# Which queue issues the writes of kept weights, of chunk 1's partial sums and of the recurrence's output: hybrid decoder step on one Trainium2 core

## Chip, cores and metric

One Trainium2 chip, one of its cores. The metric is the device time of one execution in microseconds (us); lower is better. Several executions are timed, and one more is recorded by the hardware profiler.

## What is computed

One inference step of a one-layer decoder. 1024 prompt tokens (and 64 sample tokens with a state and a cache) go through a normalisation and one joint projection into an RWKV-7 time-mixing group and a sliding-window attention group. Both outputs are gated, put side by side and projected back, then a gated per-layer embedding is added. The reference, cut to what matters:

```python
def step(S, inp):                       # RWKV-7, one token
    r_t, w_t, k_t, v_t, kk_t, a_t = inp
    sa = jnp.einsum('bhvk,bhk->bhv', S, kk_t)
    S = (S * w_t[:, :, None, :] - sa[..., None] * (kk_t * a_t)[:, :, None, :]
         + v_t[..., None] * k_t[:, :, None, :])
    return S, jnp.einsum('bhvk,bhk->bhv', S, r_t)
...
mixed = jnp.concatenate([o_r * jax.nn.silu(gate_r), o_a * jax.nn.silu(gate_a)], axis=-1)
h = h + mixed @ w_out
gate = jax.nn.sigmoid(rmsnorm(h, g_ple) @ w_pg)
h = h + gate * (p @ w_pp)
```

## The kernel before

The prompt's tokens are held as three column chunks, `CH`: 384, 384 and 320 columns (the last holds 256 prompt tokens and the 64 sample tokens). All matrix products are done in float32 with each operand split in a high and a low part, so each product is three matmuls. The kernel is written with a tile framework that puts the instructions of each engine in order itself, by a timeline that it works out before the kernel is built; a change of one operation's queue can so move others on every engine.

Up to about 520 us of the execution the joint projection and the attention run. Then `chain` lets generators take turns. `prepare` (line 772) makes, for a group of four 64-token blocks, what the recurrence needs: Gram matrices, masks, a triangular solve on VectorE (DVE; tiles `ti`, `tm`, `a`) with a detour through DRAM (`at_d`, lines 842 and 844; `tt_d`), and `TE`/`TF` (lines 883, 891), whose result ScalarE (ACT) scales into the tile `B` at line 894. `steps` (line 948) runs the recurrence block by block: matmuls at lines 962, 967, 974, 987, 990 with small DVE and ACT operations between (`rh` line 964, `sv` lines 968 and 969). `finish` (line 918) normalises a group's outputs, transposes each block's (`ytr`, line 942), copies it on ACT into a tile `or` (line 945, one buffer only) and writes that to DRAM (`or_d`, line 946): 17 writes of 128 KB, one for each of the 16 blocks of the prompt and one for the sample. The next copy at line 945 has to wait until the write before it has landed, since the tile has one buffer.

Beside this runs `Late`. Its `first` multiplies the attention half by the output weights `woa` for chunks 0 and 1; chunk 1's sums are written to `hxa` in DRAM (line 1230, eight writes of 192 KB) and loaded again later (line 1175). `second` (line 1239) does the recurrence's half with the weights `wor`, after loading `or_d` (line 1154) and `sg_d`; `gate` (line 1321) multiplies by the gate weights `wg` and the embedding weights `wpp`. A weight is loaded raw (line 143), cast to its high part `wh_..` by ACT (line 146), and its low part `wl_..` is made by GpSimd (POOL; line 55). Then `keep` (line 1301) writes both parts to DRAM at line 1304, and for a later chunk `kept` (line 1306) loads them from there (line 1309; for `wor` the load is line 1272): 16 writes for `woa` and `wor` and 16 for `wg`, all of 512 KB, and 16 for `wpp`, of 128 KB.

Every DMA of these parts goes through `DMAQ(group)` (line 87), which picks the issuing engine from the table `DQ` (line 319): "S" is SyncE (SP), "A" is ACT, and a group not in the table is "S". Before the change the table has one entry, `lp`, the three loads of `p` at lines 1164 and 1167. SP issues 615 DMAs and does nothing else.

Each queue issues in its own order, and an instruction that waits holds all behind it. The framework has eight completion semaphores for DMAs, given out in turn to all of them in the order of the program, whichever engine issues; a DMA is issued only once the one before it on the same semaphore has landed. So at most eight are under way at a time.

Of the kernel before, what the change touches and what calls it, by code (L numbers as in the profile page):

```python
# [39 lines left out]
def _build(ctx, nc, tc, A, O):  # L40
# [45 lines left out]
    global DMAQ  # L86
    DMAQ = lambda g: {"S": nc.sync, "A": nc.scalar, "P": nc.gpsimd}[DQ.get(g, "S")]
    if WARM:
# [227 lines left out]
    e.ast.close()  # L316


DQ = {"lp": "A"}
WARM = 1  # L320
TAIL = 1
RING2 = 0
# [775 lines left out]
class Late:  # L1098
# [202 lines left out]
    def keep(self, w, dst):  # L1301

        for x, d in zip(w, dst):
            DMAQ("wk").dma_start(d, self.e.f32(x))

    def kept(self, name, src, K=8, pool=None, bufs=2):
        w = [(pool or self.e.wp).tile([128, K, 128], F32R, tag=f"w{x}{K}", name=f"w{x}_{name}", bufs=bufs) for x in "hl"]
# [198 lines left out]
```

## Time and profile before

| | |
|---|---|
| time, median of 3 runs | 939.41 us (935.97 to 939.56) |
| the profiled execution | 942.16 us, its span 940.4 us |
| mean granted TensorE clock | 0.937 of full speed |
| TensorE (PE) busy | 828.5 us (88%) |
| VectorE (DVE) busy | 632.7 us (67%) |
| ScalarE (ACT) busy | 372.5 us (40%) |
| GpSimd (POOL) busy | 369.3 us (39%) |
| moved by DMA | 157.81 MB, mean 168 GB/s |

The profiled execution lies 2.75 us above the median of the three runs. An engine's busy time leaves out its DMA issues; those stand in the rows as SPq or ACTq, the sequencer of SP or ACT. "L946" is line 946. "DMA or_d<-or" is a transfer that writes `or_d` from the tile `or`, and its time in the chain of waits runs from the issue to the landing.

### The profile page before, as it was taken

The numbers are of one execution on the slowest core, as the hardware profiler recorded it, in microseconds if no ns is written. First come the engines' busy times: TensorE is split into PE (matmuls) and PEld (weight loads), VectorE is DVE, ScalarE is ACT, GpSimd is POOL, SyncE is SP. The second block draws the span as 40 slices with busy tenths as digits, with TensorE's granted clock in tenths as the row PEclk, the third lists the DMA queues.
The fourth block names the chain that finished last, engine by engine and source line by source line (L and its number), as shares of the span: only waits on it lengthen the run. The fifth ranks groups of instructions, "written<-read, shape, count | busy, mean of one in ns | idle before, by whom it ended". The sixth has DMA issues, their size and how long they took to land.

```text
span 940.4 us, 17475 instructions
## 1 busy us (share of the span) xinstructions
PE 828.5 (88%) x6352; PEld 738.4 (79%) x6352; DVE 632.7 (67%) x1511; ACT 372.5 (40%) x864; POOL 369.3 (39%) x494
## 2 busy tenths in 40 slices
PE   6978999999998989899799965987687989999994
PEld 5878999878886679788688854876577887899983
DVE  7856487777777453468774769588959766854464
ACT  6202086666666442652233332511333443322131
POOL 8548466665676422314231314315433353200000
PEclk9989999999999999899899975899797999999996
DMA  8013201322135447647644499686556879998882
GB/s 292 23 61 101 66 23 57 91 91 77 59 91 156 112 94 167 169 127 171 163 118 123 117 258 316 140 267 182 174 148 223 292 274 329 306 328 278 272 294 82
DMA packets 146007, 157.81 MB, mean 168 GB/s; under 512 B 59288, under 2 KB 115864, under 8 KB 145656
## 3 DMA queue, kind: packets, MB, share of 16 engines
q1 hardware_dynamic: 145104, 155.57, 54.6%
q10 hardware_dynamic: 816, 1.11, 0.4%
q8 instruction: 50, 0.82, 0.4%
q14 instruction: 37, 0.30, 0.1%
HBM read 106.77 MB, written 49.67 MB: 166 GB/s over the span
## 4 chain that ended last, share of the span: by engine, by line
PE 43%; DVE 25%; DMA 14%; ACT 6%; issue 6%; SPq 4%; POOL 2%; DVEq 0%; ACTq 0%; POOLq 0%
PE acc_z L157 6%; PE acc_gr L157 4%; PE acc_q L157 3%; DVE ti L55 3%; PE pp L1348 2%; DVE tm L55 2%; DMA a<-at_d 2%; ACT s L425 2%; PE ov L446 2%; PE acc_wg0g L157 1%; PE acc_wg3g L157 1%; DVE xl L58 1%; PE acc_wg7g L157 1%; PE acc_wg4g L157 1%; DVE s L421 1%
## 5 line engine op out<-in xcount | busy, mean ns | idle before, releaser
L157 PE MATMUL acc_z<-xh,wh_z 128*128 128x384 f32 (+1 forms) x312 | 65.1, 340 | 0.0
L157 PE MATMUL acc_z<-xl,wh_z 128*128 128x384 f32 (+1 forms) x312 | 62.6, 331 | 0.0
L157 PE MATMUL acc_z<-xh,wl_z 128*128 128x384 f32 (+1 forms) x312 | 62.5, 331 | 0.0
L157 PEld LDWEIGHTS acc_z<-xh,wh_z 128*128 128x128 f32 x312 | 53.7, 192 | 1.7 <-ACT pTS L505 0.2
L157 PEld LDWEIGHTS acc_z<-xh,wl_z 128*128 128x128 f32 x312 | 52.3, 188 | 1.0 <-issue 0.2
L157 PEld LDWEIGHTS acc_z<-xl,wh_z 128*128 128x128 f32 x312 | 52.6, 189 | 0.5
L55 DVE TENSOR_TENSOR ti<-ti,tm 128x56 f32<-128x56 f32 (+28 forms) x152 | 50.2, 330 | 3.5
L55 DVE TENSOR_TENSOR tm<-a,ti 128x56 f32<-128x56 f32 (+28 forms) x152 | 50.2, 330 | 3.5
L55 POOL TENSOR_TENSOR sg<-sv,GC 64x256 f32<-64x256 f32 x32 | 20.9, 652 | 63.0 <-DVE sv L55 61.1
L64 POOL TENSOR_SCALAR s<-s,sm 128x256 f32<-128x256 f32 (+1 forms) x64 | 34.6, 557 | 17.2 <-ACT pT L444 4.6
L1187 ACT ACTIVATE q<-hx 128x384 f32<-128x384 f32 (+1 forms) x41 | 20.8, 507 | 51.8 <-DVE hx L55 19.4
L800 PE MATMUL gram<-L,K 64*128 64x128 f32 x272 | 31.4, 324 | 4.9 <-issue 3.3
L55 POOL TENSOR_TENSOR wl_z<-wr_z,wh_z 128x1024 fp32r<-128x1024 f32 x13 | 31.3, 2406 | 10.1 <-ACT wh_z L146 4.8
L800 PEld LDWEIGHTS gram<-L,K 64*128 64x128 f32 x272 | 27.0, 219 | 9.5 <-issue 6.5
L55 DVE TENSOR_TENSOR zr<-acc_z,R 128x384 f32<-128x384 f32 (+2 forms) x52 | 21.7, 434 | 18.5 <-PE acc_z L157 18.2
L55 DVE TENSOR_TENSOR sq<-sq,q 128x384 f32<-128x384 f32 (+1 forms) x41 | 22.6, 552 | 15.1 <-ACT q L1187 14.7
L425 ACT ACTIVATE s<-s,sm 128x256 f32<-128x256 f32 (+1 forms) x64 | 30.9, 485 | 1.9 <-DVE sm L62 1.9
L446 PE MATMUL ov<-pT,vtok 128*64 128x512 f32 x60 | 31.2, 638 | 0.4 <-ACT pT L444 0.4
L1358 ACT ACTIVATE t<-t 128x384 f32<-128x384 f32 (+3 forms) x25 | 12.2, 494 | 46.8 <-DVE t L55 46.8
L55 POOL TENSOR_TENSOR gsa<-gsa,goa 128x384 f32<-128x384 f32 (+1 forms) x12 | 11.8, 985 | 45.8 <-DVE ti L55 27.0
L804 ACT COPY B<-L 64x512 f32<-64x512 f32 x34 | 20.9, 616 | 20.8 <-DVE L L55 19.9
L55 DVE TENSOR_TENSOR L<-gram,cst 128x512 f32<-128x512 f32 x34 | 22.5, 684 | 8.2 <-PE gram L800 8.0
(622 smaller groups left out, 2445.7 us busy)
## 6 DMA issues: line engine op xcount, KB each, us to landing
wr_z<-in_wz SPq DMA_DIRECT2D x13, 512.0 KB
L<-kq_d SPq DMA_DIRECT2D x24, 256.0 KB
sv<-vt_d SPq DMA_DIRECT2D x32, 128.0 KB
wh_wo<-wo_dh SPq DMA_DIRECT2D x8, 512.0 KB
wl_wo<-wo_dl SPq DMA_DIRECT2D x8, 512.0 KB
raw<-in_xT SPq DMA_DIRECT2D x8, 384.0 KB
kq_d<-KQ SPq DMA_DIRECT2D x8, 384.0 KB
bk_d<-BK SPq DMA_DIRECT2D x8, 384.0 KB
```

Of the source, the lines that this page charges most:

```text
L55: e.tensor_tensor(out, a, b, op=op)
L58: V.scalar_tensor_tensor(out, a, s, b, op0, op1)
L64: e.tensor_scalar(out, a, s1, s2, op0, op1)
L157: PE.matmul(acc[:, :n], w_[:, k0 + k, :], a_[c][:, k, :n], start=i + k == 0, stop=i == 2 and k == K - 1)
L421: V.tensor_tensor_reduce(s[:, j, :nk], sc[:, jj, :nk], mask, 1.0, -3e38, ADD, MAX, mx[:, j:j + 1])
L425: S.activation(s[:, j, :nk], s[:, j, :nk], AF.Exp, bias=m[:, 0, j:j + 1], accum_out=m[:, 2, j:j + 1])
L446: PE.matmul(ov[own, :], vtok[:, blk, own], pT[g].rearrange("p a b -> p (a b)"), start=pos == 0, stop=pos == nb - 1)
L800: PE.matmul(Gp[h][:, p], bk[hs, p], L[h][hs, p], start=True, stop=True)
L804: S.copy(r.B[hs, ci], L[h][hs])
L1187: e.S.square(q, h)
L1348: PE.matmul(pa, w[:, i], p[:, i], start=i + j == 0, stop=i == 1 and j == len(pr) - 1)
L1358: S.activation(t, t, AF.Tanh, scale=0.5)
```

## The change

Three groups of DMAs get the entry "A" in the table: `xs` (line 1230), `or` (line 946) and `wkw`, a new name that the writes at line 1304 get in place of `wk`. The loads that kept the name `wk` (lines 1272 and 1309) stay on SP.

```diff
-DQ = {"lp": "A"}
+DQ = {"lp": "A", "wkw": "A", "xs": "A", "or": "A"}
...
         for x, d in zip(w, dst):
-            DMAQ("wk").dma_start(d, self.e.f32(x))
+            DMAQ("wkw").dma_start(d, self.e.f32(x))
```

73 DMAs go from SP to ACT: 48 at line 1304, 8 at line 1230, 17 at line 946. What is computed, and every byte that is moved, stays. The order of the engines up to about 535 us of the execution stays too; behind that it changes on all five.

SP's order around 534 to 548 us of the execution, where the first four outputs of the recurrence are written (`L_` are loads of keys and queries, `sv_` of values, `at_d` and `a_2` the solve's detour):

```order
 L903 DMA sv_5176<-vt_d 64x2x256 x2
-L946 DMA or_d_3664<-or_4773 512x1x64
-L788 DMA L_3688<-kq_d 64x2x512
-L842 DMA at_d_3675<-B_3690 32x16x32 x3
-L946 DMA or_d_3664<-or_4785 512x1x64
-L842 DMA at_d_3675<-B_3690 32x16x32
+L788 DMA L_3688<-kq_d 64x2x512
+L842 DMA at_d_3675<-B_3690 32x16x32 x4
 L937 DMA bvl_5348<-vt_d 128x256
 L937 DMA bvl_5360<-vt_d 128x256
 L793 DMA K_3685<-bk_d 128x2x512
-L946 DMA or_d_3664<-or_4797 512x1x64
```

The writes of `or_d` are gone from SP, and the loads and the writes of `at_d` follow each other directly.

ACT's order at the same place:

```order
 L945 COPY or_4773<-ytr_4770 128x256
 L804 COPY B_3690<-L_3688 64x512
+L946 DMA or_d_3664<-or_4773 512x1x64
 L297 ACTIVATE gtr_6768<-gsr_6767 128x320
 L914 ACTIVATE yq_5140<-y_5135 128x256
 L945 COPY or_4785<-ytr_4782 128x256
+L946 DMA or_d_3664<-or_4785 512x1x64
 L297 ACTIVATE gtr_6799<-gsr_6798 128x320
 L945 COPY or_4797<-ytr_4794 128x256
+L946 DMA or_d_3664<-or_4797 512x1x64
```

Each write now stands behind its own copy on the engine that made it.

ACT's order about 660 to 680 us, where the last group of blocks (12 to 15) of the prompt gets ready for the recurrence (`es` is taken from `TE`, and line 894 makes `B` from `TF`; `sv_5882` is block 12's):

```order
 L886 COPY es_5589<-TE_5590 32x512 x2
-L914 ACTIVATE yq_5846<-y_5841 128x256
-L1136 CAST mrh_7757<-or_7769 128x384
-L894 ACTIVATE B_3686<-TF_5627 32x16x32 x2
-L1136 CAST mrh_7757<-or_7769 128x384
-L819 COPY K_6819<-ktr_6847 128x512
-L914 ACTIVATE yq_5908<-y_5903 128x256
-L968 ACTIVATE sv_5882<-ch_7134 64x256
 L1184 ACTIVATE sq_7781<-hx_6823 128x384
 L1199 ACTIVATE uh_7779<-hx_6823,par 128x384
 L146 CAST wh_wor4c_7876<-wr_wor4c_7874 128x1024
```

and the rows that follow these:

```order
+L1304 DMA wo_dh<-wh_wor4c_7876 128x2x512
+L1187 ACTIVATE q_7823<-hx_6823 128x384
+L1199 ACTIVATE uh_7779<-hx_6823,par 128x384
+L894 ACTIVATE B_3686<-TF_5627 32x16x32 x2
 L945 COPY or_5937<-ytr_5934 128x256
+L946 DMA or_d_3665<-or_5937 512x1x64
+L968 ACTIVATE sv_5882<-ch_7134 64x256
```

Line 894 stood right behind `es` and ahead of the cast of `wor4`; now it stands behind that cast and behind a write of its result.

## Rows read from the trace of the kernel before

**Rows 1.** The page: busy time by engine, and the chain's shares.

```profile
PE 828.5 (88%) x6352; PEld 738.4 (79%) x6352; DVE 632.7 (67%) x1511; ACT 372.5 (40%) x864; POOL 369.3 (39%) x494
...
PE 43%; DVE 25%; DMA 14%; ACT 6%; issue 6%; SPq 4%; POOL 2%; DVEq 0%; ACTq 0%; POOLq 0%
```

**Rows 2.** Windows: length, busy PE, PEld, DVE, ACT, POOL, clock, DMA share, GB/s.

```profile
560.00:600.00 40.00, 27.00 (x174) 23.26 (x174) 34.71 (x85) 17.10 (x37) 17.84 (x24) 0.62 0.85 257
...
800.00:860.00 60.00, 57.45 (x351) 54.40 (x351) 37.31 (x89) 17.36 (x38) 9.18 (x13) 1.00 0.91 311
```

**Rows 3.** Timeline of SP's queue from 534 to 548 us: start, us.

```profile
536.10 0.56 SPq L946 DMA_DIRECT2D or_d<-or  x1
...
540.00 0.55 SPq L946 DMA_DIRECT2D or_d<-or  x1
...
542.83 0.56 SPq L946 DMA_DIRECT2D or_d<-or  x1
...
545.47 0.60 SPq L844 DMA_DIRECT2D a<-at_d  x1
...
547.38 0.55 SPq L946 DMA_DIRECT2D or_d<-or  x1
```

**Rows 4.** Chain of waits from 530 to 560 us: start, us, what.

```profile
536.10 3.41 DMA or_d<-or
...
540.00 2.30 DMA or_d<-or
...
545.47 4.86 DMA a<-at_d
...
558.30 5.42 DMA hx<-in_xT
```

**Rows 5.** The chain from 560 to 700 us.

```profile
564.83 9.06 DMA wo_dh<-wh_woa
573.90 5.08 DMA sv<-vt_d
...
598.46 0.53 SPq L946
...
612.91 0.42 SPq L1230
...
691.57 0.55 SPq L946
```

**Rows 6.** Lines 946, 1304 and 1230: issue, ns min/median/max, first and last start.

```profile
L946 SPq DMA_DIRECT2D or_d<-or x17: 524/552/1444, 536.1 to 785.6; - x17
...
L1304 SPq DMA_DIRECT2D wo_dl<-wl_woa x4: 377/394/460, 568.0 to 626.8; - x4
...
L1304 SPq DMA_DIRECT2D wg_dh<-wh_wg0g x1: 333/333/333, 716.6 to 716.6; - x1
...
L1230 SPq DMA_DIRECT2D hxa<-xr x8: 327/418/1217, 609.5 to 656.3; - x8
```

**Rows 7.** Waits of SP's queue from 500 us: in total, times, longest.

```profile
SPq L1304 <- ACT wh_wor4c L146: 9.3, 1, 9.3
...
SPq L903 <- DMA wo_dh<-wh_woa: 2.2, 2, 1.6
```

**Rows 8.** Waits of ACT from 500 us.

```profile
ACT or L945 <- DMA or_d<-or: 11.7, 7, 2.2
```

**Rows 9.** Waits of PE from 560 to 590 us.

```profile
PE ytr L942 <- DVE y L55: 5.2, 1, 5.2
PE acc_wa L157 <- DVE mal L55: 3.3, 2, 2.4
PE gram L800 <- issue: 3.3, 1, 3.3
```

**Rows 10.** Timeline of ACT from 645 to 712 us.

```profile
666.61 1.19 ACT L894 ACTIVATE B<-TF 32x512 f32<-32x512 f32 x2
...
678.24 1.03 ACT L146 CAST wh_wor4c<-wr_wor4c 128x1024 fp32r<-128x1024 f32 x1
```

## The prediction

> **What bounds the kernel now.** I read the page first: PE is busy for 88% of the span and holds 43% of the chain of waits, DVE 25%, transfers 14%, ACT 6%, SP's own queue 4% [rows 1]. So no engine that the change touches is the bound over the whole; what the change is worth has to come from stretches. The windows show which. Before about 535 us nothing is reordered. From 800 to 860 us PE is busy for 57.45 of 60 us at full clock [rows 2]: what comes earlier there is only worth something if it was late before. From 560 to 600 us PE is busy for 27.0 of 40, the granted clock is 0.62, and the transfers take 0.85 of the DMA engines at 257 GB/s [rows 2]: there PE starves. The chain of waits then shows what is late in such stretches. Around 540 us it runs through the writes of `or_d` and on through SP's queue to a load of `a` at 545.47, and at 558.30 it passes to a load of `hx` [rows 4]; then it stands on transfers of 9.06 and 5.08 us [rows 5]. From there to 700 us it is mostly DVE and PE, with single issues of SP in between [rows 5]. The reader is to see that SP matters in a few places, for a few tenths of a microsecond to two microseconds each, and bytes in one.
>
> **The change part by part.** 73 DMAs move, none is added, no byte is saved. At the durations that SP needs for them, with one row standing for its group, this is 17 x 0.552 + 8 x 0.418 + 16 x 0.394 + 32 x 0.333 = 29.7 us of issue that leaves SP and comes to ACT [rows 6]. ACT is busy for 372.5 us of 940 [rows 1], so it has room; but it is an engine on whose order others wait, SP is not.
>
> *The train around 540 us.* The load of `a` at 545.47 is in the chain [rows 4], and SP issues back to back from 536 to 546 us; ahead of it stand three writes of `or_d`, at 536.10, 540.00 and 542.83, with 0.56, 0.55 and 0.56 us [rows 3] and some 0.07 us from one issue to the next. All three leave: 1.67 + 0.2 = 1.9 us earlier, **-1.9**. The fourth write, at 547.38, stands behind the load and counts for nothing. What the load releases (DVE, then SP's train to the load of `hx` at 558.30) shifts along. Were something else late next, as the landing of the `at_d` writes in the same train, nothing would be gained: bounds 0 and -1.9. I take the whole, since these writes follow each other closer too once the first two are gone.
>
> *The writes of `or_d` themselves.* The single buffer makes each copy at line 945 wait for the write before it, 11.7 us in 7 waits [rows 8]. The first write landed after 3.41 us among SP's loads, the next after 2.30 us [rows 4]. On ACT a write is issued right behind its copy. I count the difference once, **-1.1**, because only around 540 us do these landings stand in the chain with PE behind them; bounds 0 and -11.7.
>
> *Later single issues.* In the chain SP's issue of a moved write stands at 598.46, 612.91 and 691.57 us, with 0.53, 0.42 and 0.55 us [rows 5]. They leave SP's queue, and the load or write behind each comes earlier by as much: **-1.5**. At 691.57 the issue is on the way to a load too, so the gain holds whoever issues the write; bounds 0 and -1.5.
>
> *The first weights kept.* From 564 to 576 us the four parts of `woa` are written among loads. SP's loads of values (line 903) wait for a `wo_dh` write to land, 2.2 us in two waits [rows 7], because the completion semaphore comes round to them. The eight semaphores stay, so a wait of this kind can only be dealt out afresh. I take half, **-1.1**; bounds 0 and -2.2.
>
> *ACT.* The added issues and what they wait for hold all behind them. Issue alone: 29.7 us, of which what lies on the path counts. The nearest row is ACT's share of the chain, 6% [rows 1]: 0.06 x 29.7 = **+1.8**; bounds 0 and +29.7. The largest wait that SP had for a moved write was 9.3 us for the cast of `wor4` [rows 7]; on ACT that cast stands right ahead of the write, so this wait vanishes instead of moving. Writes of low parts wait for POOL, and on ACT that holds casts and copies; the windows show POOL with 17.84 of 40 us busy where it is fullest of the two shown [rows 2], and I count nothing more for it, bounds 0 and one copy of a low part.
>
> *The new order.* From 654 to 760 us all engines get another order. I take 0: PE's work is the same, and what is put later makes room for weights' products put earlier. The bounds are rival two's price on one side and, on the other, the PE waits that could close.
>
> Sum: -1.9 - 1.1 - 1.5 - 1.1 + 1.8 = **-3.8 us**. The profiled execution took 942.16 us, 2.75 above the median of 939.41; it would come to 938.4, and from the median the forecast is **935.6 us** (-0.4%). A measurement of this kernel tells about 0.5%, or 4.7 us, from no change.
>
> **The rivals.** *One: nothing arrives.* Bytes and the eight semaphores bound the stretch from 560 to 600 us, PE and DVE the rest, so what SP saves is waited for elsewhere and ACT's cost eats the remainder. For it: 0.85 of the DMA engines busy [rows 2] and the small share of SP in the chain [rows 1]. Against it: the train of 536 to 546 us, where the queue itself is back to back [rows 3]. Time: 939.4 with some 2 us either way.
>
> *Two: slower, by ACT's order.* The last four blocks of the prompt cannot begin until line 894 has made `B`. It ran at 666.61 us; the cast of `wor4`, which now stands ahead of it, ran at 678.24 us and took 1.03 [rows 10], since it waits for PE to be done with earlier weights. If the cast does not come earlier, line 894 starts 678.24 + 1.03 + 0.39 - 666.61 = 13.1 us later, with the write's issue in it [rows 6, 10], and the recurrence's last four blocks with it. Against the gain of 3.8 this gives +9.3, so 948.7. It decides the sign once more than 3.8 us of those 13.1 reach the end, and is told from no change once 8.5 do. For it: the recurrence is serial, and everything of the third chunk waits for its output. Against it: PE gets products of `wor` to do meanwhile, which bring the cast forward, and DVE's solve, not PE, holds the chain there for much of the time.
>
> *Three: a larger gain.* Where PE starved from 560 to 590 us it waited 5.2 + 3.3 + 3.3 = 11.8 us for data made from loads [rows 9]. The loads stand behind 512 KB writes on SP; four of those are 2.1 MB, 8.2 us at the 257 GB/s of that stretch [rows 2]. If on a queue of their own the writes no longer delay the loads, up to that comes on top: 935.6 - 8.2 = 927.4. Against it: the DMA engines are 0.85 busy, so writes take the bytes' time from the loads whichever queue they are on, and loads issued just before a write are slowed instead.
>
> The Trainium skill, DMA: Bandwidth & Descriptors, bears on this third rival with two rules. In the section Issuing engines are not separate DMA queues it says that transfers started by different engines run on the same 16 DMA engines and interleave, and that starting them from several engines only saves the sequencer's time; by that the third rival falls, and the sum keeps its issue terms alone. The section Queues, rings and completion order says that SP and ACT each own a ring on every one of those DMA engines, which takes turns between them by packets; by that a load would no longer stand wholly behind a write. No row of the kernel before shows two full queues side by side, so neither is borne out yet, and I leave the third rival the smaller chance.
>
> **How the numbers follow.** Chances: the forecast 0.37, with its own range 932.5 to 939; rival one 0.20; rival two 0.26; rival three 0.17. That is about 0.19 of the forecast, 0.01 of rival one and all of rival three for faster by over 0.5%; 0.17 of the forecast, 0.18 of rival one and 0.02 of rival two within 0.5%; 0.01, 0.01 and 0.24 for slower. So faster 0.37, same 0.37, slower 0.26. The range leaves out the far half of rival two and little of rival three: 926 to 948 us.
>
> **What would show it.** If right, in the changed profile: SP's queue passes from line 903 to the load of `a` about 2 us earlier around 545 us; the writes of `or_d` land in some 2.3 us; the stretch to 654 us, where orders barely differ, gains some 4 us; ACT's row of busy time hardly moves and its issue rows at lines 946, 1230 and 1304 show the durations that SP had. Rival three would show a higher PE share and clock from 560 to 600 us. Rival two would show line 894's last full-width pair some 10 us later than 666.61 and PE idle behind it for `ch` or `cs`, not made up by 800 us. A saving in the first 535 us, or a stretch after 800 us that differs by more than 3 us on its own, would mean that I looked in the wrong place; the forecast is wrong as a whole if the gain to 654 us is absent while SP's train is shorter.

## The result and the profile after

The changed kernel takes 945.41 us (median of 20 runs, 940.62 to 952.04) against 940.98 us for the kernel before on the same chips: 1.0052 times as long, 95% interval 1.0036 to 1.0068. The prediction was a slight gain, 935.6 us. The profiled execution took 946.4 us, its span 944.6 us, with a mean granted clock of 0.928 (before: 0.937).

The page of the changed kernel, busy time by engine and the chain's shares:

```profile
PE 834.9 (88%) x6352; PEld 745.0 (79%) x6352; DVE 640.2 (68%) x1511; ACT 373.3 (40%) x864; POOL 371.6 (39%) x494
...
PE 45%; DVE 24%; DMA 14%; ACT 6%; issue 5%; SPq 3%; POOL 3%; DVEq 0%; ACTq 0%; POOLq 0%
```

Against [rows 1] hardly a share moves: SP's queue goes from 4% to 3% of the chain, PE from 43% to 45%. A page does not show this loss; the stretches do. Its windows, for the two of [rows 2]:

```profile
560.00:600.00 40.00, 27.84 (x226) 24.13 (x225) 34.64 (x83) 18.09 (x39) 17.86 (x24) 0.62 0.91 267
800.00:860.00 60.00, 59.89 (x354) 54.62 (x353) 43.09 (x98) 18.91 (x41) 12.60 (x14) 1.00 0.96 332
```

From 560 to 600 us nothing much is different, and from 800 us on PE is fuller than before. The loss lies between. The window that shows it, and a later one, with the same columns (length, busy PE, PEld, DVE, ACT, POOL, clock, DMA share, GB/s), first of the kernel before:

```profile
735.00:765.00 30.00, 26.62 (x157) 23.84 (x156) 23.28 (x46) 11.13 (x22) 15.73 (x16) 0.94 0.93 318
810.00:870.00 60.00, 57.45 (x362) 56.82 (x361) 33.29 (x72) 17.60 (x39) 7.83 (x11) 1.00 0.88 299
```

and of the changed one:

```profile
735.00:765.00 30.00, 21.54 (x185) 19.56 (x184) 17.16 (x40) 7.92 (x18) 8.26 (x10) 0.77 0.56 191
810.00:870.00 60.00, 59.89 (x367) 56.95 (x366) 38.33 (x91) 17.12 (x38) 8.99 (x12) 1.00 0.93 316
```

From 735 to 765 us the changed kernel leaves PE idle for 8.5 us, at a granted clock of 0.77, and the DMA engines are at 0.56 instead of 0.93. What both wait for is the end of the recurrence. SP's next loads there are chunk 1's sums (`hxa`, line 1175), which stand on SP behind the write of the recurrence's last state `so` (line 982). SP's queue before:

```profile
734.50 0.34 SPq L982 DMA_DIRECT2D out_wkvp<-so  x1
...
739.30 1.75 SPq L1175 DMA_DIRECT2D hx<-hxa  x4
```

and after:

```profile
746.46 0.34 SPq L982 DMA_DIRECT2D out_wkvp<-so  x1
751.02 1.75 SPq L1175 DMA_DIRECT2D hx<-hxa  x4
```

The write comes 12.0 us later, the loads 11.7. In the changed kernel's chain of waits (start, us, what) this stretch runs through a write of a kept weight, a load of `bvl` (values that `finish` adds) and chunk 1's first and second product with `wor` (`acc_wr0c`, `acc_wr1c`):

```profile
730.23 6.10 DMA wg_dl<-wl_wg1g
...
736.86 4.40 DMA bvl<-vt_d
...
745.97 4.14 PE acc_wr0c L157 x12
...
754.88 4.18 PE acc_wr1c L157 x12
```

The first product in the chain before, and the start of the second in PE's timeline before:

```profile
734.00 2.31 PE acc_wr0c L157 x12
```

```profile
744.02 1.16 PE L157 MATMUL acc_wr1c<-mrh,wh_wor0c 128*128 128x384 f32 x4
```

The ends of some groups of matmuls, in us, follow one chain through the stretch ("q" is the queue alone, a run told of below):

| end of | before | after | q |
|---|---|---|---|
| the first transpose of `finish`, line 942 | 533.2 | 532.3 | 533.1 |
| block 7, line 974 | 562.2 | 559.6 | 559.4 |
| `TE` of the last four blocks, line 883 | 662.4 | 667.7 | 658.1 |
| block 13, line 974 | 692.1 | 700.3 | 687.6 |
| block 14, line 962 | 713.9 | 733.8 | 706.0 |
| block 15, line 974 | 734.0 | 746.0 | 727.2 |
| chunk 1's first product of `wor` | 736.3 | 750.1 | 729.4 |
| the third chunk's first of `wor` | 817.5 | 823.5 | 810.5 |
| the third chunk's last of `wor` | 877.0 | 881.6 | 874.3 |
| the last product of all | 921.0 | 925.8 | 917.9 |

The changed kernel comes to this part 0.9 us earlier, by nothing that was changed; it is 2.5 us ahead at 560 us, 20 us late at block 14, 12 us late at block 15, and 5 us late at the end.

The issues themselves cost on ACT what they had cost on SP [rows 6], or a little less. The view of lines 946, 1304 and 1230 after:

```profile
L946 ACTq DMA_DIRECT2D or_d<-or x17: 520/521/592, 533.7 to 792.4; - x17
...
L1304 ACTq DMA_DIRECT2D wo_dl<-wl_woa x4: 366/372/392, 569.0 to 626.0; - x4
...
L1230 ACTq DMA_DIRECT2D hxa<-xr x8: 338/350/1600, 599.9 to 651.7; - x8
```

And line 894 stands where the second rival put it. ACT's timeline after:

```profile
674.05 1.03 ACT L146 CAST wh_wor4c<-wr_wor4c 128x1024 fp32r<-128x1024 f32 x1
675.12 0.37 ACTq L1304 DMA_DIRECT2D wo_dh<-wh_wor4c  x1
678.59 0.52 ACT L1187 ACTIVATE q<-hx 128x384 f32<-128x384 f32 x1 [3.50 <-DVE hx L55]
...
679.64 1.20 ACT L894 ACTIVATE B<-TF 32x512 f32<-32x512 f32 x2
```

It starts 13.0 us later than in [rows 10]; the rival had said 13.1. Whether that makes the loss is what the experiments had to tell.

### The profile page after: what moved, and what is told of

Same layout as the page of the kernel before. It is cut to its first block, busy times and chain, and to the rows that moved or that the text cites. A ratio compares the mean times of both kernels' runs of the same rounds, so it can differ in the third digit from the quotient of the medians.

```text
span 944.6 us, 17446 instructions
## 1 busy us (share of the span) xinstructions
PE 834.9 (88%) x6352; PEld 745.0 (79%) x6352; DVE 640.2 (68%) x1511; ACT 373.3 (40%) x864; POOL 371.6 (39%) x494
## 4 chain that ended last, share of the span: by engine, by line
PE 45%; DVE 24%; DMA 14%; ACT 6%; issue 5%; SPq 3%; POOL 3%; DVEq 0%; ACTq 0%; POOLq 0%
PE acc_z L157 6%; PE acc_gr L157 5%; DVE ti L55 3%; PE acc_q L157 3%; DVE tm L55 2%; DMA a<-at_d 2%; PE pp L1348 2%; ACT s L425 2%; DMA K<-bk_d 2%; PE ov L446 2%; PE gram L800 2%; PE acc_wg0g L157 2%; PE acc_wg7g L157 1%; PE acc_wg5g L157 1%; PE acc_wg3g L157 1%
## 5 line engine op out<-in xcount | busy, mean ns | idle before, releaser
L55 DVE TENSOR_TENSOR tm<-a,ti 128x56 f32<-128x56 f32 (+28 forms) x152 | 52.2, 343 | 3.4
L55 DVE TENSOR_TENSOR ti<-ti,tm 128x56 f32<-128x56 f32 (+28 forms) x152 | 52.1, 343 | 3.4
L55 DVE TENSOR_TENSOR sq<-sq,q 128x384 f32<-128x384 f32 (+1 forms) x41 | 26.0, 635 | 14.6 <-ACT q L1187 14.0
L55 POOL TENSOR_TENSOR gsa<-gsa,goa 128x384 f32<-128x384 f32 (+1 forms) x12 | 11.7, 972 | 45.7 <-DVE gsa L58 14.3
```

The costliest lines, as they stand in the source:

```text
L55: e.tensor_tensor(out, a, b, op=op)
```

## The experiments

**How an order is held.** Two things came with the edit: another queue for 73 DMAs, and another order on every engine. To part them, a function gives each instruction a dependency on the one before it on its engine, by a table of instruction numbers. Such a dependency sets the order and adds no wait:

```diff
+def _pin(nc, tc):
...
+        if e in last:
+            tc.add_manual_dep(i, last[e], mybir.DependencyInfo(mybir.DependencyClass.NoSync, mybir.DependencyReason.DATA),
+                              reason="order")
+        last[e] = i.name
...
+        _pin(nc, tc)
```

Below, "order" in a diff stands for that table. Ratios are to the kernel before, with their 95% intervals.

### Queue and order apart

```diff
 DQ = {"lp": "A", "wkw": "A", "xs": "A", "or": "A"}
-order: the changed one
+order: before's
```

> All 73 writes issued by ACT as in the changed kernel, but every engine keeps the order of the kernel before (the writes stand on ACT where they stood in the program). Theory 'order' (the new order of all engines, with line 894 behind the cast of wor4 and the last four blocks late, costs the time; ACT as issuer gains a little): 935 to 939 us, ratio to before 0.994 to 0.998. Rival 'queue' (ACT's added issues and waits hold back what stands behind them): 944 to 947 us, ratio 1.004 to 1.007, with PE late by 4 us or more behind ACT.

939.42 us, 0.9985 (0.9964 to 1.0006). The reverse, all writes on SP in the changed order:

```diff
-DQ = {"lp": "A", "wkw": "A", "xs": "A", "or": "A"}
+DQ = {"lp": "A"}
 order: the changed one
```

> All writes on SP as before, but every engine keeps the order of the changed kernel. Theory 'order': as slow as the changed kernel or slower, 945 to 949 us, ratio 1.004 to 1.009, with the last four blocks some 10 us late at 720 to 750 us. Rival 'queue': as fast as before, 939 to 942 us, ratio 0.998 to 1.002.

946.09 us, 1.0063 (1.0037 to 1.0089). The queue costs nothing; the order costs the whole loss and a little more: 1.0052 / 0.9985 = 1.0067, some 6.3 us. With all writes on SP the order costs 1.0063. The table stands in the run that is divided by in the first figure and in the run itself in the second, so that they agree leaves no cost of its own to the table. In the traces each engine's order is the one that was pinned, but in the first run 51 of the 618 DMAs complete on another of the eight semaphores than before.

The three groups of writes, each in before's order:

```diff
-DQ = {"lp": "A", "wkw": "A", "xs": "A", "or": "A"}
+DQ = {"lp": "A", "or": "A"}
```

> Only the 17 writes of the recurrence's output on ACT, order of the kernel before. Theory 'order' with the terms of the prediction (train around 540 us -1.9, landing -1.1, single issues -1): 937 to 939 us, ratio 0.996 to 0.998. Rival 'queue': these writes cost ACT 9.4 us of issue, ratio 1.000 to 1.003.

938.74 us, 0.9979 (0.9961 to 0.9996).

```diff
+DQ = {"lp": "A", "xs": "A", "or": "A"}
```

> The writes of the recurrence's output and of chunk 1's partial sums on ACT, the kept weights' writes on SP, order of the kernel before. If the groups' effects add up as read so far (output alone 0.998, kept weights alone 1.0025, all three 0.9985) the partial sums are worth about -0.002: ratio 0.994 to 0.998, 934 to 938 us. If they don't add (noise between orders of semaphores): 0.997 to 1.001.

937.66 us, 0.9972 (0.9951 to 0.9994).

```diff
+DQ = {"lp": "A", "wkw": "A"}
```

> Only the 48 writes of kept weights on ACT, order of the kernel before. Theory 'order': 939 to 942 us, ratio 0.998 to 1.001, since the prediction gave them -1.1 and two thirds of ACT's 1.8. Rival 'queue': they carry most of the cost by their waits for POOL and for landings: 943 to 946 us, ratio 1.003 to 1.006.

943.94 us (937.37 to 946.25), 1.0025 (1.0000 to 1.0049): no gain, and wider spread than the others; its one profile (span 936.5 us) does not show why. So the output's writes carry the gain, chunk 1's sums add little that can be told, and the kept weights' writes, 48 of the 73, add none to the time. The first two of these three versions beat the kernel before, by 0.2 to 0.3%, and the changed one by more.

### Where in the changed order the loss is made: cuts

All writes on ACT, before's order up to a point and the changed order behind it:

```diff
-order: the changed one
+order: before's up to the cut, the changed one behind it
```

Cut at the last four blocks' first transpose (656 us):

> 73 writes on ACT; the order of the kernel before up to the last four blocks' first transpose (about 659 us), the changed kernel's order for all that then remains. Theory 'the loss lies behind 656 us': as slow as the changed kernel, ratio 1.003 to 1.007. Rival 'the changed orders ahead of it cost': ratio 0.997 to 1.000.

943.11 us, 1.0028 (1.0003 to 1.0052).

Cut behind block 12's second step (670 us), which puts line 894 back in its place:

> As the run before, but with the old order only up to the second matmul step of block 12 (670 us in the kernel before): line 894 is early, the rest of blocks 12 and 13 is in the changed order, DVE's too. Theory 'PE's queue': as the run cut at block 13, 1.001 to 1.005. Rival 'blocks 12 and 13 by DVE's order': slower than the run cut at block 13 by 0.003 or more. Had line 894 alone been it, 0.995 to 0.999 (already against the run with blocks 12 and 13 put early).

945.68 us, 1.0055 (1.0030 to 1.0081).

Cut behind block 13's third step (692 us):

> 73 writes on ACT; the order of the kernel before up to the third matmul step of block 13 (692 us in the kernel before), then the changed kernel's order, in which blocks 14 and 15 stand behind the products of wg0 and wg1 on PE and chunk 1's first product of wor behind block 15. Line 894 and blocks 12 and 13 run early, on all engines. Theory 'PE's queue' (blocks 14 and 15 behind the gate's products): ratio 1.001 to 1.005, chunk 1's first product of wor late by 8 us or more against the run with the old order throughout. Rival 'blocks 12 and 13' (the loss is made when they are late, by line 894 and by DVE's order): ratio 0.995 to 0.999.

948.14 us, 1.0084 (1.0055 to 1.0113).

Cut behind the sample's block (708 us):

> 73 writes on ACT; the order of the kernel before up to the second matmul step of the sample's block (lines 1041 and 1046, 708 us in the kernel before), then the changed kernel's order, with blocks 14 and 15 behind the products of wg0 and wg1 on PE. Theory 'the sample's block' (it uses the same PSUM banks as blocks 14 and 15 and comes before them; in the changed order it is 17 us late on PE, ACT and DVE): ratio 0.996 to 1.001, far better than the run cut at block 13 (1.0084). Rival 'what follows it' (blocks 14 and 15 behind the gate's products, and DVE's order there): 1.004 to 1.009, as the run cut at block 13.

944.75 us, 1.0038 (1.0015 to 1.0062).

Cut behind block 15's third step (734 us):

> 73 writes on ACT; the order of the kernel before up to the third matmul step of block 15 (734 us in the kernel before), the changed kernel's order for all that then remains. Theory 'the loss is made between 656 and 735 us': ratio 0.996 to 1.000, as with the old order throughout. Rival 'the later order costs too': ratio 1.002 or more.

938.69 us, 0.9971 (0.9948 to 0.9994). With line 894 and block 13 back in place the loss is still there, and no smaller; with all up to block 15 back it is gone. What the changed order does behind 734 us costs nothing. The cuts behind block 12, block 13 and the sample's block each came out between or above the figures of their theories, so none of the theories named so far (line 894, PE's queue, the sample's block) fits them all. Two more cuts divide the last piece, behind block 14's first step and behind its third:

> All 73 writes on ACT; before's order up to and with block 14's first step alone (line 962), the changed order behind it. If the place of the first step on PE (7.3 us of gate products that stand ahead of it) is what holds block 14: its first step near 708 us, its second (line 967) near 710, and 0.997 to 1.000. If what holds block 14 is the rest of its chain, on DVE (rh, sv behind the normalisations) and PE (second step behind the gate's products): second step still 725 us or later, and 1.002 to 1.004.

943.02 us, 1.0035 (1.0007 to 1.0062).

> All 73 writes on ACT; before's order up to and with block 14's third step (line 974, near 715 us), the changed order behind it. The cut after the sample's block gave 1.0038 and the cut after block 15's third step 0.9971, so 0.67% (6.3 us) hang on what lies between. Theory A, block 14 itself (in the changed order its first step stands behind all of wor's products and the gate's first two parts): nearly all of it comes back, 0.997 to 0.999, block 14's third step near 716 us and block 15's near 730 us. Theory B, block 15 (DVE does block 14's normalisation and the sample's bvl ahead of block 15's rh and sv, and bvl's load on SP stands behind a kept weight's load): 1.002 to 1.004, block 14's third step near 716 us but block 15's still 735 us or later.

944.27 us, 1.0046 (1.0024 to 1.0068). Here block 14's third step ends at 713.7 us (before: 722.3, with the queue alone 715.1), and block 15's at 741.5 (before: 734.0, with the queue alone 727.2). So block 14 is not it, and theory B of that expectation points the right way: VectorE's order around block 15. Its timeline in this run (start, us, what, and the idle time before with its releaser):

```profile
729.28 0.56 DVE L55 TENSOR_TENSOR t<-acc_wg1g,R 128x384 f32<-128x384 f32 x1 [2.51 <-PE acc_wg1g L157]
...
731.23 0.55 DVE L58 SCALAR_TENSOR_TENSOR hx<-t,hx 128x384 f32<-128x384 f32 x1
731.70 0.86 DVE L55 TENSOR_TENSOR sv<-cs,sg 64x256 f32<-64x256 f32 x2
736.92 0.42 DVE L55 TENSOR_TENSOR bvl<-bvl,bq 128x256 f32<-128x256 f32 x1 [4.36 <-DMA bvl<-vt_d]
737.38 0.42 DVE L964 COPY rh<-ch 128x256 f32<-128x256 f32 x1
...
739.91 0.43 DVE L969 TENSOR_SCALAR sv<-ch 64x256 f32<-64x256 f32 x1
741.55 0.42 DVE L55 TENSOR_TENSOR so<-cs,sg 128x256 f32<-128x256 f32 x1 [1.21 <-PE cs L974]
```

Block 15's input `sv` could be made at 714 us, but stands behind the gate's second update (`t`, `hx`), which waits for products on PE; then `rh` stands behind block 13's `bvl`, for whose load DVE waits 4.36 us. SP's queue shows why that load is late:

```profile
726.57 0.38 SPq L1272 DMA_DIRECT2D wh_wor2c<-wo_dh  x1
...
732.10 0.38 SPq L1272 DMA_DIRECT2D wl_wor2c<-wo_dl  x1
732.57 0.42 SPq L937 DMA_DIRECT2D bvl<-vt_d  x1
```

It stands behind the load of a kept weight. In the changed kernel itself that load of a weight waits for a write to land which ACT has issued, since the eight completion semaphores go round all engines. SP's waits from 690 to 765 us after:

```profile
SPq L982 <- DVE so L55: 9.1, 1, 9.1
...
SPq L1272 <- DMA wg_dl<-wl_wg1g: 4.1, 1, 4.1
```

### Single pieces moved

Block 15's three steps and block 14's output alone into before's place, from the cut behind block 14 (`ch_7320` is block 15's bank, `acc_wg0g` and `acc_wg1g` are the gate's products on PE):

```diff
 L157 MATMUL acc_wg0g_0_8067<-ul_7780,wh_wg0g_8061 128x384 x8
...
-L157 MATMUL acc_wg1g_0_8130<-uh_7779,wl_wg1g_8125 128x384 x8
-L942 MATMUL ytr_7127<-cst,y_7097 128x128 x2
+L157 MATMUL acc_wg0g_0_8067<-uh_7779,wl_wg0g_8062 128x384 x4
 L962 MATMUL ch_7320<-sv_7291,L_3683 64x64
```

> As order_old_to_block14 (1.0046; block 15's third step ends at 741.5 us), but block 15's own three steps, block 14's output steps and its mean stand where before's order has them: on TensorE behind 20 of the gate's first 24 products instead of behind all of these and the second part's, on VectorE ahead of the gate's second update, on ScalarE and GpSimd likewise; SP's order is not touched. If block 15's lateness makes the loss: its third step near 730 us and 0.997 to 0.999. If it is something else in what the changed order does behind block 14 (loads, weights' products, later DVE order): block 15's third step near 730 us, but 1.002 to 1.005.

944.98 us, 1.0050 (1.0031 to 1.0070). Block 15's third step ends at 726.9 us, and the loss stays. Its last output `so`, though, is as late as ever, because on DVE it stands behind the same `bvl`. DVE and SP in this run:

```profile
746.57 0.43 DVE L55 TENSOR_TENSOR bvl<-bvl,bq 128x256 f32<-128x256 f32 x1 [4.05 <-DMA bvl<-vt_d]
...
747.24 0.42 DVE L55 TENSOR_TENSOR so<-cs,sg 128x256 f32<-128x256 f32 x1
```

```profile
742.09 0.38 SPq L1272 DMA_DIRECT2D wl_wor2c<-wo_dl  x1
742.56 0.42 SPq L937 DMA_DIRECT2D bvl<-vt_d  x1
```

So the last run moves two instructions more: that load, and the addition on DVE that frees its buffer (`y_7097` and `bvl_7123` are the sample's):

```diff
 L1272 DMA wh_wor2c_8166<-wo_dh 128x2x512
+L937 DMA bvl_7411<-vt_d 128x256
 L1331 DMA wpp3g_8254<-in_wpp 128x256
 L1272 DMA wl_wor2c_8167<-wo_dl 128x2x512
-L937 DMA bvl_7411<-vt_d 128x256
...
+L55 TENSOR_TENSOR y_7097<-y_7097,bvl_7123 128x256
 L55 TENSOR_TENSOR t_8155<-acc_wg1g_0_8130,R_7782 128x384
 L58 SCALAR_TENSOR_TENSOR t_8155<-t_8155,pp_8156 128x384
-L55 TENSOR_TENSOR y_7097<-y_7097,bvl_7123 128x256
```

> As block15_early (1.0050), with two instructions moved besides: VectorE's last addition to the sample's output (it frees a buffer of bvl) ahead of the gate's second update instead of inside it, and SP's load of block 13's bvl ahead of the load of wor2's low part, which waits 3.1 us on a semaphore. In block15_early this load was issued at 742.56 us, VectorE waited 4.05 us for it, and so (which frees the bank for the second product of chunk 1, acc_wr1c) came at 747.24, acc_wr1c at 753.05 us. If that wait is what is left of the loss: load issued near 739, so near 743.7, acc_wr1c near 749.5 us, and 3.6 us or 0.4% less, 1.000 to 1.002. If the wait is only one of several that end together: so and acc_wr1c earlier by the same, but the time within 0.1% of 1.005.

941.39 us, 1.0016 (0.9995 to 1.0037), as expected of the first case; the interval overlaps a little with that of the run before (1.0031 to 1.0070). DVE in this run:

```profile
741.54 0.43 DVE L55 TENSOR_TENSOR bvl<-bvl,bq 128x256 f32<-128x256 f32 x1 [1.95 <-DMA bvl<-vt_d]
...
742.21 0.41 DVE L55 TENSOR_TENSOR so<-cs,sg 128x256 f32<-128x256 f32 x1
```

`so` is 5.0 us earlier, chunk 1's second product `acc_wr1c` begins at 747.63 instead of 753.05 us, and the last product of all ends at 918.9 us, as in the cut behind block 15 (918.8); in `block15_early` it was 924.8. Not all of the 5.0 is the wait for `bvl`: the moved addition also lets PE's transpose `ytr`, which waited 2.1 us for it, pass, and 1.0 us is there at block 15's third step already (725.9 against 726.9). The load and the addition were not moved one without the other.

Four runs put pieces elsewhere. `TE`, line 894 and blocks 12 and 13 early in the changed order:

```diff
-order: line 894 behind the cast of wor4
+order: line 894 and the steps of blocks 12 and 13 in before's place
```

> The changed kernel (73 writes on ACT) in its own order, with one piece put back where it stands in the kernel before: TE, es, TF and line 894 of the last four blocks and the steps of blocks 12 and 13 that hang on them, so that line 894 comes ahead of the cast of wor4 again. Blocks 14 and 15 stay behind the gate weights' products on PE. Theory 'line 894' (the order costs because line 894 comes 13 us late): 938 to 942 us, ratio 0.997 to 1.001. Rival 'PE's queue' (the order costs because blocks 14 and 15 stand behind the products of wg0 and wg1 on PE, and chunk 1's products of wor behind block 15): line 894 is back near 667 us, yet 943 to 947 us, ratio 1.003 to 1.007.

950.07 us, 1.0098 (1.0065 to 1.0131). Line 894 ends at 670.1 us and still block 12's third step only at 691.0, because DVE's order holds block 12's `sv`:

```profile
687.50 0.43 DVE L969 TENSOR_SCALAR sv<-ch 64x256 f32<-64x256 f32 x1
```

The gate's products behind blocks 14 and 15:

```diff
-order: PE's second half of wg0 and wg1 ahead of block 14
+order: the same behind block 15
```

> The changed kernel in its own order with one thing put back: the products of wg0 (its tail) and wg1, with the DVE and ACT operations that take them out of PSUM, stand behind blocks 14 and 15 again, where the kernel before has them. Line 894 and blocks 12 and 13 stay late. Theory 'PE's queue' (blocks 14 and 15, and chunk 1's first product of wor, stand behind the gate's products): that first product comes some 10 us earlier than in the changed kernel, ratio 0.998 to 1.002. Rival 'the sample's block' (blocks 14 and 15 cannot start before the sample's block is through, which is late as well; the gate's products only fill the wait): ratio 1.003 to 1.006, as the changed kernel.

953.18 us, 1.0130 (1.0099 to 1.0162). Block 14's first step comes only 3.6 us earlier (730.2); what it waits for now is DVE, so the products ahead of it had in the main filled a wait. PE's waits from 690 to 765 us:

```profile
PE acc_wr2c L157 <- DMA wh_wor2c<-wo_dh: 4.6, 1, 4.6
PE ch L962 <- DVE y L55: 4.2, 1, 4.2
```

Both at once:

```diff
+order: the gate's products late, and the chain of blocks 12 to 15 early
```

> As the run before, and besides it the last four blocks and the sample's block (TE, es, TF, line 894 and the recurrence's steps) put early where the old order allows; what remains keeps the changed kernel's order. Theory 'PE's queue': no more than the run before, 0.997 to 1.002. Rival 'the sample's block': this one recovers where the run before doesn't, 0.997 to 1.001. If both stay at 1.003 or more, the loss hangs on what else is ordered anew between 692 and 735 us.

959.01 us, 1.0201 (1.0165 to 1.0238): a miss for both theories. And the reverse, before's order with the sample's block alone put late, behind the products of `wor`'s last part:

```diff
-order: the sample's block ahead of block 14
+order: the sample's block behind the products of wor7
```

> 73 writes on ACT and the order of the kernel before, but the sample's block (its TE, TF, line 894, lines 1041 to 1046) stands behind the products of wor7 as in the changed kernel, and what needs its banks behind it. Line 894 of the last four blocks and blocks 12 and 13 stay early. Theory 'the sample's block': 1.003 to 1.008 with blocks 14 and 15 late by 10 us or more. Rival 'what follows it': 0.996 to 1.001, as the old order throughout (0.9985).

951.94 us, 1.0125 (1.0086 to 1.0164); block 15's third step ends at 740.2 us. So a late sample's block costs too, in the old order. Its loss is not that of the recurrence's end: `so` comes at 740.2 us here and at 739.9 in the cut behind block 15, which loses nothing. Pieces of an order do not add: all four mixtures are worse than either whole.

## Why the prediction was wrong

**The reading of the bound** holds: the stretches named are those that starve, SP matters in a few places, and the forecast's gain to 654 us is there. With the queue alone, `TE` of the last four blocks ends 4.3 us earlier (662.4 to 658.1), where some 4 us to 654 was forecast. That the size fits is in part luck, since of its terms the first two were not there, as follows. Over the whole kernel the queue alone is worth 1.4 us (0.9985; from 3.4 less to 0.6 more) instead of 3.8.

**The train around 540 us, -1.9.** The sum of this term failed, by its own lower bound. With the queue alone the load of `a` is issued at 545.17 instead of 545.47 [rows 3], after a start of the train 0.2 us earlier. What is late next is the landing of an `at_d` write, the case that the prediction had named for its bound 0. In the chain of the changed kernel:

```profile
537.84 4.73 DMA at_d<-B
...
544.49 4.83 DMA a<-at_d
```

**The fourth write, counted for nothing.** At 547.38 [rows 3] it stands ahead of the loads of `rn` (line 837), for which DVE waits, and there a gain was made. DVE's timeline before, and then with the queue alone:

```profile
556.21 0.18 DVE L62 TENSOR_SCALAR rn<-rn 128x32 f32<-128x32 f32 x1 [2.08 <-DMA rn<-ss_d]
```

```profile
554.01 0.18 DVE L62 TENSOR_SCALAR rn<-rn 128x32 f32<-128x32 f32 x1 [0.52 <-DMA rn<-ss_d]
```

This is 2.2 us earlier, and block 7's third step, which comes behind it on DVE and ACT, 2.7 us earlier. But the place in the queue is not what gained it: SP waits ahead of these two loads for DVE, 1.2 us before and 1.7 with the queue alone. SP's rows before, and then with the queue alone:

```profile
551.60 1.78 SPq L837 DMA_DIRECT2D rn<-ss_d  x2
```

```profile
550.96 1.11 SPq L837 DMA_DIRECT2D rn<-ss_d  x2
```

They start 0.6 us earlier, and the second of them takes 0.59 us to issue instead of 1.27; the rest lies behind the issue. That moving the `or_d` writes makes the gain is shown by all twenty traces. In the three with these writes on SP the second load takes 0.90 to 1.27 us to issue, and from the first transpose of `finish` to block 7's third step it is 28.9 to 29.1 us; in the seventeen with them on ACT it is 0.59 to 0.60 and 25.8 to 27.9 us. Which of the writes it is, and how a write makes these loads slower, was not tried. The chain of waits of [rows 4] ran through the load of `hx` at this place, so it did not show this one.

**The landing of `or_d`, -1.1.** Wrong. In the changed kernel ACT issues the second of these writes at 537.72, and the next copy begins at 542.42 us, after a wait of 2.74 us for it. Such waits come to 11.1 us with the queue alone and in the changed kernel to no less than in [rows 8]:

```profile
ACT or L945 <- DMA or_d<-or: 13.6, 6, 4.8
```

**Later single issues, -1.5,** are right in sign: with the queue alone the lead at the end of `TE` grows from 1.8 us (603 us) to 4.3 (662). **The first weights kept, -1.1:** not seen in the time (`wkw_only_order_old`, 1.0025), though in that run's one trace the stretch from block 7's third step to `TE` of the last four blocks takes 97.8 us instead of 100.2. It is 98.5 with the `or_d` writes alone and 98.6 with all, so these two terms can't be told apart. **ACT, +1.8,** could not be measured by itself.

**The new order, "I take 0".** This is the step that failed. It measured +6.3 us (1.0067), more than all the gains together. The reason given, that what is put later makes room for products put earlier, counts PE's work. What counts is what the recurrence's end releases. Chunk 1's products of `wor` take turns with `ch` and `cs` in the same two PSUM banks, so the first needs the bank of block 15's `ch`, and the second that of its `cs`, which is free only when `so` and the block's output have been taken out of it; and SP's loads of chunk 1's sums stand behind the write of `so`. The changed order puts three things ahead of block 15's last operations and of `so`: the gate's second update, a load of `bvl` that itself stands behind a kept weight's load, and the sample's last addition. Putting block 15's steps, that load and the addition back takes 1.0046 to 1.0016, and before's order as far as block 15 takes it to 0.9971.

**Why 20 us late becomes 5.** Between block 14's first step and block 15's third, 8 of the 20 us are made up. `acc_wr1c` then starts 10.9 us late (754.88 against 744.02), and from there to the last product of all it is 170.9 us in the changed kernel, 176.9 before and 180.7 with the queue alone. In ten of the twenty traces, this one included, it is 169.9 to 171.7 and in none less: some 171 us (an estimate from these ten) is what the work behind takes in these orders when it waits for little. So the kernel before had about 6 us to spare behind the recurrence, and what is late by more comes out at the end: 10.9 less 6.0 is 4.9 us. That is also why the cut behind block 15 loses nothing, with `so` 12.7 us and `acc_wr1c` 7.8 us later than with the queue alone. Part of the lateness is PE's clock: PE was busy for 2.10 of the 5 us from 737 to 742, and behind that the granted clock was 0.50 (1.2 GHz) from 745.9 to 750.1 us, so the first product took 4.14 us; before, at 1.00 (2.4 GHz), it took 2.31.

From 765 to 870 us PE in the changed kernel is full (44.57 of 45 us and 59.89 of 60). Before, and more so with the queue alone, it waits there for loads of kept weights. PE's waits from 800 to 880 us, before:

```profile
PE acc_wg1g L157 <- DMA wh_wg1g<-wg_dh: 1.5, 1, 1.5
PE acc_wr3c L157 <- DMA wh_wo<-wo_dh: 1.1, 1, 1.1
```

and with the queue alone:

```profile
PE acc_wg2g L157 <- DMA wh_wg2g<-wg_dh: 2.8, 1, 2.8
PE acc_wr2c L157 <- DMA wh_wo<-wo_dh: 1.2, 1, 1.2
```

So the queue's lead of 7.0 us at 817 us is 2.7 at 877, and the run is not told from no change when timed (0.9985). That is **rival one**, at another place than it had named: bytes and semaphores take back what SP saved.

**Rival two** had the side and the price of line 894 (13.0 us against 13.1), and 948.7 us for 945.4. That the time came near was luck, since its mechanism is not the cause: with line 894 back in place the loss was 1.0055, and with it early in the changed order 1.0098. **Rival three** fell: from 560 to 600 us DMA share and GB/s go from 0.85 and 257 to 0.91 and 267 (0.88 and 269 with the queue alone), PE's busy time from 27.0 to 27.84 us, and the clock stays at 0.62. The Trainium skill, DMA: Bandwidth & Descriptors, section Issuing engines are not separate DMA queues, says that starting transfers from several engines saves only the sequencer's time. These figures agree with it.

Still open: how the 0.45% between `block15_and_bvl_early` and the cut behind block 15 divides, if it is real at all (the intervals overlap and the profiles end alike); why the kept weights' writes alone spread so widely; and how the loss divides among the earlier cuts. The profiles of the cuts at 656 us and behind block 14's first step were taken of executions 3.8 and 2.2 us faster than their medians, and hardly show the loss that was timed (the last product ends at 917.7 and 919.8 us).

## What to carry to other kernels

In a framework that works out the order itself, a change of one queue is two changes: hold the old order and try the queue, hold the queue and try the order, before either is judged. A changed order is priced at what the late step releases next (a load behind it on a queue, a bank behind it), less what the engines behind it have to spare, not at the work of the engine that stays busy meanwhile. When a loss hides in an order, cuts between the two whole orders find it; mixtures of pieces mislead.

## What the runs showed of the hardware that was not expected

A write issued by ACT held SP: its load at line 1272 waited 4.1 us for `wg_dl` to land. With the same order and all writes on SP it waited 3.1 us for the same write, so a queue of its own does not part two trains that share the eight semaphores. A write of `or_d` takes about as long to issue on ACT (0.521 us) as on SP (0.552 in [rows 6]), and nothing here shows it landing sooner: in the changed kernel's chain of waits such writes stand around 690 us with 4.68, 2.23 and 2.40 us, against 3.41 and 2.30 around 540 us in [rows 4]. But a load issued on SP near such a write was issued faster once the write stood on ACT (0.59 us against 0.90 to 1.27).
